# Own tile pools for meta tokens and rotary queries, the latents' ends behind the next projection's first products, the FFN norm's squares through PSUM

## The chip, the cores and the metric

The kernel runs on one core of one Trainium2 chip. The metric is the device time of the core in microseconds (us), from the program's first to its last instruction and what lies around it; the time before is the median of three runs.

## What is computed

One layer of an encoder with two token mixers. 1024 tokens and 16 learned meta tokens (1040 rows of width 1024, float32) pass a mixer and a gated feed-forward net (FFN):

```python
proj = u @ w_in
rq, rk, rv, rg, a_cq, a_ckv, a_kr, a_gret, a_gmla = jnp.split(proj, SPLIT_IDX, axis=-1)
y_ret = (silu(rg) * group_norm(bidir_retention(rope(rq), rope(rk), rv))) @ w_ret_out
c_q  = rmsnorm(a_cq, q_norm_w);   q = c_q @ w_uq            # 384-wide latent, 8 heads of 64 + 32 rotary
c_kv = rmsnorm(a_ckv, kv_norm_w); k_nope = c_kv @ w_uk; v = c_kv @ w_uv    # 256-wide latent
k_rope = rope(a_kr)                                          # one 32-wide key for all heads
y_mla = softmax_attention(q, [k_nope, k_rope], v) @ w_mla_out
merged = sigmoid(a_gret) * y_ret + sigmoid(a_gmla) * y_mla
h = h + merged @ w_o
h = h + (silu(u2 @ w_gate) * (u2 @ w_up)) @ w_down           # u2 = rmsnorm(h), d_ff = 2816
out = rmsnorm(h)[:, 16:]
```

## The kernel before

Everything lies with channels on the 128 partitions and tokens along the free axis. A float32 product is made of three matmuls on operands split into a high and a low part (hi·hi, hi·lo, lo·hi; lines L137 to L139, L217). The parts are made by ScalarE (the high copy, L209, L153, L275) and VectorE (the difference, L210, L154, L276).

**Units of seven products.** A product of 256 weight columns pairs with the two token halves goes by seven instead of eight block products (`seven`, `seven_out`; names 11, t2, t3, n1, 21, t4, 22). GpSimd makes the weights' sums (L191 to L193, L207), ScalarE and VectorE split them (L209, L210), TensorE runs 12 matmuls of 128x512 for each of the seven, and VectorE adds the PSUM banks up (L234 to L242). A unit has 84 matmuls. There are four banks (`pm`) for these products, so the next unit's t2 needs the bank of this unit's t2 read out.

**Stages the change touches**, in order of time: the units that make the values; those of the shared key and the third query latent (`project_key` on `win(22)`), of the key-value latent (`project_kv` on `win(20)`), and a gate unit of which one product was made at the start (`rest_gates`: it loads that from `e_d`, L813, and adds it at L302); then four units of the retention's output (`ret_out(0)` to `ret_out(3)`, on `Z`, whose blocks are loaded and split one by one at L839, L275, L276), which multiply by a gate that they load from `g_d` (`ret_post`, L856, L857) and store to `r_d` (L858). Around `ret_out(1)` and the third unit the rotary part of the queries is made: 36 matmuls from the normed query latents `cq` (loaded at L909), then the rotation on VectorE (L893 to L898). Within `ret_out(3)` the first pair of heads begins (`heads_k`, L973).

A latent's end is what follows its unit: the meta tokens' values, which gather in a PSUM tile of their own, are summed (`meta_sum`, L432), transposed on TensorE (L779 for the key-value latent, L802 for the shared key), split and stored (`latent_part`, L730, L732 to L734; `shared_key`, L755 to L763), and the sum of squares `lss` goes over the partitions by matmuls with ones (L160) into the norm's factor (`latent_norm`, L741 to L744).

Tiles of 128x512 come from a rotating pool `cr` of six slots: the units' sums, the meta tokens' small tiles (16 columns) and the rotary tiles alike.

**Output projection** (`w_o`): for each half c of the tokens and each of eight row blocks m, 24 matmuls (L137 to L139), the residual add from PSUM (L1216), and, for c = 1, the FFN's input blocks (L1229, L1234, L1236 on GpSimd, L1239, splits at L154). The square of the new residual is made by ScalarE (L1245) and added to `ssum` by GpSimd (L1246). `norm(c)` sums `ssum` over partitions by matmuls with ones (L1197). The FFN's first gate unit starts with nine matmuls of each of its first four products, which need row blocks 0 to 5 alone, and the last three of each follow.

Instructions keep their order on each engine; between engines they wait on semaphores. The order is made by the framework's scheduler from the order of the program and its priorities, and all DMAs of this kernel are issued from one queue, SP's, in order; an issue that waits holds the ones behind it.

## Time and profile before

| | us |
|---|---|
| median of three runs (1775.68 to 1776.03) | 1775.89 |
| the profiled execution, its own time | 1780.81 |
| its span, first to last instruction | 1779.0 |
| TensorE busy in it | 1714.6 (96%) |
| VectorE busy | 1339.0 (75%) |
| ScalarE busy | 861.1 (48%) |
| GpSimd busy | 790.1 (44%) |

The profile is of one execution. TensorE (PE) is busy for nearly all of it, so a shorter time comes from its idle stretches and from stretches in which its granted clock (PEclk, as a share of 2.4 GHz) was below 1. DVE is VectorE, ACT ScalarE, POOL GpSimd, SP the engine whose queue issues DMAs. A busy TensorE issues a 128x512 matmul every 0.22 to 0.23 us at full clock; the 0.39 us that a row shows is the time one spends in the pipeline.

### The profile page before, as it was taken

The page shows a single profiled execution, that of the slowest core. Times are in us where ns is not written, and L with a number is a line of the kernel's source. Part 1 is how long each engine was busy: PE and PEld are TensorE (multiplying, and loading weights), DVE is VectorE, ACT ScalarE, POOL GpSimd, SP SyncE. Part 2 cuts the span into 40 slices and gives each one's busy share as a digit, 9 for nine tenths or more (in the row PEclk, how much of TensorE's full clock was granted, in tenths as well). Part 3 has the DMA queues.
Part 4 walks back from the last instruction along what each step waited for, and adds up shares of the span by engine and source line. Part 5 has one row for each costly group of instructions (what it writes and reads, how often), then busy time and mean ns, then how long its engine had stood idle before and what let it go on. Part 6 is the DMA issues. An engine that isn't in the chain of part 4 may idle for free.

```text
span 1779.0 us, 26433 instructions
## 1 busy us (share of the span) xinstructions
PE 1714.6 (96%) x8804; PEld 1443.9 (81%) x8804; DVE 1339.0 (75%) x2448; ACT 861.1 (48%) x1614; POOL 790.1 (44%) x605
## 2 busy tenths in 40 slices
PE   8999999999999899999999999899999999999997
PEld 6788777788887677899998888788888888787787
DVE  7845778788888857888888758767666666987965
ACT  7425766344324523788787346433332232543434
POOL 1322257674554321234332524666676566533422
PEclk9999999999999899999999999999999999999999
DMA  7733823566546785111112754233323333854512
GB/s 255 240 101 119 295 85 117 180 201 213 189 158 230 213 301 179 28 34 40 30 59 69 231 187 162 66 101 119 101 95 101 107 105 101 286 176 123 154 57 95
DMA packets 145433, 253.59 MB, mean 143 GB/s; under 512 B 18889, under 2 KB 36738, under 8 KB 145298
## 3 DMA queue, kind: packets, MB, share of 16 engines
q1 hardware_dynamic: 145298, 251.92, 43.5%
q8 instruction: 69, 1.13, 0.3%
q14 instruction: 66, 0.54, 0.1%
HBM read 174.93 MB, written 76.85 MB: 142 GB/s over the span
## 4 chain that ended last, share of the span: by engine, by line
PE 49%; DVE 7%; DMA 3%; ACT 3%; issue 2%; SPq 0%; POOL 0%; DVEq 0%; ACTq 0%; POOLq 0%
PE mm L217 29%; PE o L1041 3%; PE mm L138 3%; PE mm L137 3%; PE mm L139 3%; PE t L1012 2%; DVE slot L154 2%; PE s L137 1%; PE s L138 1%; PE s L139 1%; DMA slot<-g_d 1%; DMA slot<-f_d 1%; DVE slot L210 1%; DVE ptl L1015 1%; PE o L137 1%
## 5 line engine op out<-in xcount | busy, mean ns | idle before, releaser
L217 PE MATMUL mm<-slot,slot 128*128 128x512 f32 x2604 | 598.3, 392 | 8.4 <-ACT slot L209 3.7
L217 PEld LDWEIGHTS mm<-slot,slot 128*128 128x128 f32 x2604 | 490.6, 189 | 115.0 <-DVE slot L210 5.5
L209 ACT CAST slot<-slot 128x512 fp32r<-128x512 f32 (+1 forms) x413 | 246.1, 598 | 465.9 <-PE mm L217 395.0
L210 DVE TENSOR_TENSOR slot<-slot,slot 128x512 fp32r<-128x512 f32 (+1 forms) x413 | 361.6, 877 | 71.5 <-ACT slot L209 70.4
L217 PE MATMUL mm<-ht,slot 128*128 128x512 f32 x648 | 219.6, 400 | 7.4 <-DVE slot L210 3.4
L217 PE MATMUL mm<-h,slot 128*128 128x512 f32 x536 | 184.4, 403 | 0.0
L191 POOL TENSOR_TENSOR slot<-slot,slot 128x512 f32<-128x512 f32 (+1 forms) x61 | 85.3, 1398 | 220.0 <-DMA slot<-in_w_u 50.7
L207 POOL TENSOR_TENSOR slot<-slot,slot 128x512 f32<-128x512 f32 (+1 forms) x61 | 84.7, 1390 | 185.1 <-DVE slot L210 173.1
L217 PEld LDWEIGHTS mm<-ht,slot 128*128 128x128 f32 x648 | 122.1, 190 | 35.1 <-DVE slot L210 5.6
L154 DVE TENSOR_TENSOR slot<-slot,slot 128x512 fp32r<-128x512 f32 x137 | 117.5, 872 | 20.6 <-ACT slot L153 20.0
L217 PE MATMUL mm<-lt,slot 128*128 128x512 f32 x324 | 128.7, 397 | 0.0
L153 ACT CAST slot<-slot 128x512 fp32r<-128x512 f32 x137 | 83.3, 619 | 76.9 <-DMA slot<-f_d 30.3
L192 POOL TENSOR_TENSOR slot<-slot,slot 128x512 f32<-128x512 f32 (+1 forms) x61 | 86.0, 1410 | 77.6 <-DVE slot L210 65.6
L217 PEld LDWEIGHTS mm<-h,slot 128*128 128x128 f32 x536 | 101.2, 190 | 21.6 <-DVE slot L210 0.6
L1002 DVE TENSOR_SCALAR_CACHE_REDUCE pr<-s,sq_c 128x384 f32<-128x384 f32 (+1 forms) x192 | 103.3, 573 | 7.9 <-PE t L1020 3.8
L217 PE MATMUL mm<-l,slot 128*128 128x512 f32 x268 | 106.6, 398 | 0.0
L139 PE MATMUL mm<-slot,slot 128*128 128x512 f32 (+1 forms) x288 | 105.3, 366 | 0.0
L138 PE MATMUL mm<-slot,slot 128*128 128x512 f32 (+1 forms) x288 | 105.3, 366 | 0.0
L137 PE MATMUL mm<-slot,slot 128*128 128x512 f32 (+1 forms) x288 | 105.1, 367 | 0.0
L1015 DVE TENSOR_TENSOR ptl<-t,pth 128x512 fp32r<-128x512 f32 x128 | 85.7, 685 | 18.2 <-ACT pth L1014 17.6
L1046 POOL TENSOR_TENSOR oa<-oa,ob 64x256 f32<-64x256 f32 x32 | 24.0, 751 | 154.5 <-ACT ob L1045 149.1
L193 POOL TENSOR_TENSOR slot<-slot,slot 128x512 f32<-128x512 f32 (+1 forms) x61 | 88.2, 1445 | 1.4
(365 smaller groups left out, 3506.0 us busy)
## 6 DMA issues: line engine op xcount, KB each, us to landing
slot<-in_w_in SPq DMA_DIRECT2D x106, 256.0 KB
f_d<-slot SPq DMA_DIRECT2D x71, 256.0 KB
slot<-f_d SPq DMA_DIRECT2D x71, 256.0 KB
slot<-in_xT SPq DMA_DIRECT2D x48, 256.0 KB
slot<-z_d SPq DMA_DIRECT2D x44, 256.0 KB
slot<-in_w_g SPq DMA_DIRECT2D x44, 256.0 KB
slot<-in_w_u SPq DMA_DIRECT2D x44, 256.0 KB
slot<-in_w_dq SPq DMA_DIRECT2D x48, 192.0 KB
```

What stands on the lines that cost most here:

```text
L137: pe.matmul(ps, sh, mh, start=start, stop=False)
L138: pe.matmul(ps, sh, ml, start=False, stop=False)
L139: pe.matmul(ps, sl, mh, start=False, stop=stop)
L154: dve.tensor_sub(lo, t, f(hi))
L191: pool.tensor_add(s1, a21, a22)
L192: pool.tensor_sub(s2, s1, a11)
L193: pool.tensor_sub(a21, a21, a11)
L209: act.copy(hi, side[b])
L210: dve.tensor_sub(low, side[b], f(hi))
L217: pe.matmul(ps, sw[:, ks], sx, start=begins and q == qs[0] and i == 0, stop=q == nq - 1 and i == 2, skip_group_check=True)
L1002: dve.tensor_scalar(pr[:, c], ps[:, :n], sq_c[:, qb : qb + 1], None, ALU.mult, ALU.max, accum_out=mx[:, j : j + 1])
L1015: dve.tensor_sub(pt[1][d], tp, f(pt[0])[d])
```

## The change

1. The meta tokens' tiles of up to 16 columns and their sums get pools of their own (`small`, 8 tiles; `sums`, 2 tiles); the rotary tiles get `rotary_r` (11 slots). `cr` keeps its six slots.
2. The end of the shared key's unit is written behind the products 11 and t2 of the key-value unit, that unit's end behind t2 and n1 of the gate unit.
3. The query latents' loads are tied to earlier stores; the key-value latents' tiles `ckv` and the factor row `skv_b` are opened and loaded after the third unit (in memory that the rotary pools leave), where they were loaded with the query latents before; a GpSimd memset goes.
4. For `w_o`, the squares go to a PSUM bank of the pool `pm` and are added by VectorE (14 adds move from GpSimd), the difference L1236 moves from GpSimd to VectorE (4), `norm(0)` is written after both halves, and `norm(1)` after the first 36 matmuls of the FFN's first unit.

```diff
@@ prod: products already written are not written again
-        banks, w, begun = {}, {}, []
+        banks, w, begun, done = {}, {}, [], set()
         def prod(b, qs=range(nq)):
             k = BANK[b]
+            qs = [q for q in qs if (b, q) not in done]
+            done.update((b, q) for q in qs)
@@ small tiles of the meta tokens
+        small, sums = sb(mid, "small", 8, side="right"), sb(mid, "sums", 2, side="right")
+        def work(n):
+            return slot(cr) if n > NM else mk(small, (P, NM), "small")
         def meta_sum(ps, lo, n):
-            t = slot(cr)[:NM, :n]
+            t = mk(sums, (P, 256), "sums")[:NM, :n]
...
         def latent_part(t, c, dst, col, first):
-            hi = slot(cr, F32R)[:, :n]
+            hi = work(n).bitcast(F32R)[:, :n]
...
@@ ends of the latents
         tail = slice(S, L)
+        pending = []
+        def after_pending(prod, names=("t2", "n1")):
+            if pending:
+                for b in names:
+                    prod(b)
+                pending.pop()()
+            return prod
         def project_kv():
...
-            seven_out(seven(w7, win(20), U, (ps, M1 | M2)), cr, post)
-            t = meta_sum(ps, 0, 256)
-            pt = mk(pc, (P, 512), "mm")
-            for k in range(2):
-                pe.transpose(pt[:, k * NM : k * NM + NM], t[:, k * P : k * P + P], ident[:NM, :NM])
-                latent_part(pt[:, k * NM : k * NM + NM], tail, ckv_d[k], column(C_KVN + k), k == 0)
-            latent_norm(skv_c, 2, 1.0, range(NB + 1))
+            seven_out(after_pending(seven(w7, win(20), U, (ps, M1 | M2)), ("11", "t2")), cr, post)
+            def rest():
+                t = meta_sum(ps, 0, 256)
...
+                latent_norm(skv_c, 2, 1.0, range(NB + 1))
+            pending.append(rest)
...
-            seven_out(seven(w7, win(22), U, (ps, M2)), cr, post)
-            t = meta_sum(ps, P, 48)
...
+            seven_out(after_pending(seven(w7, win(22), U, (ps, M2))), cr, post)
+            def rest():
+                t = meta_sum(ps, P, 48)
...
+                latent_norm(sq_c, 3, 96.0**-0.5, range(NB))
+            pending.append(rest)
...
         def rest_gates(i):
             e = slot(cr)
             load(e, e_d[i])
-            rest_out([(seven(w7, win(12 + i), U), e, gate_post(g_d, 2 * i))], cr)
+            rest_out([(after_pending(seven(w7, win(12 + i), U)), e, gate_post(g_d, 2 * i))], cr)
@@ rotary queries
-        ckv = [tuple(mk(ap, (P, 1152), f"ck{j}{k}", F32R)[:, :L] for j in "hl") for k in range(2)]
-        swp = sb(right, "skv", 1, side="right")
-        skv_b = mk(swp, (P, L), "skv_b")
-        fill(swp, 112)
...
+        rr_ = sb(rot, "rotary_r", 11, side="right")
...
-            ta, tb_ = slot(cr), slot(cr)
+            ta, tb_ = slot(rr_), slot(rr_)
...
-        for i, (dst, src) in enumerate([(t, cq_d[k][j]) for k in range(3) for j, t in enumerate(cq[k])] + [
-                (t, ckv_d[k][j]) for k in range(2) for j, t in enumerate(ckv[k])]):
-            with tc.issue_after(issued[1 + i * 3 // 5].ins):
+        for i, (dst, src) in enumerate([(t, cq_d[k][j]) for k in range(3) for j, t in enumerate(cq[k])]):
+            with tc.issue_after(issued[1 + i // 2].ins):
                 load(f(dst), src)
...
-        load(skv_b, n_d.rearrange("b i -> (b i)")[:L].unsqueeze(0).broadcast_to([P, L]))
...
         rot.close()
+        ap = sb(right, "latent_kv", 1, side="right")
+        ckv = [tuple(mk(ap, (P, 1152), f"ck{j}{k}", F32R)[:, :L] for j in "hl") for k in range(2)]
+        swp = sb(right, "skv", 1, side="right")
+        skv_b = mk(swp, (P, L), "skv_b")
+        load(skv_b, n_d.rearrange("b i -> (b i)")[:L].unsqueeze(0).broadcast_to([P, L]))
+        for k in range(2):
+            for j, t in enumerate(ckv[k]):
+                load(f(t), ckv_d[k][j])
         ret_out(3)
@@ output projection and the FFN's first unit
-                    pool.tensor_sub(g12, g12, g22)
+                    dve.tensor_sub(g12, g12, g22)
...
-                    t = slot(xr)
+                    t = mk(pm, (P, 512), "mm")
                     act.square(t, hm)
-                    pool.tensor_add(ssum[c], ssum[c], t)
-            norm(c, slice(0, 512))
+                    dve.tensor_add(ssum[c], t, ssum[c])
+        norm(0, slice(0, 512))
...
             if j == 0:
                 for b in NAMES[:4]:
                     prod(b, range(3))
-                    rest[b] = range(3, 4)
+                norm(1, slice(0, 512))
```

Three places in the order of the instructions. **TensorE between the gate unit and `ret_out(0)`**: `mm_1158` (`mm_1183` after) holds the key-value latent's transposed meta tokens, `mm_1164` (`mm_1189` after) the sums over `lss`, `mm_1191` is the gate unit's bank for t3, and `mm_1283` and `mm_1286` (`mm_1277` after) are banks of `ret_out(0)`. Before, behind `ret_out(0)`'s product 11:

```order
L217 MATMUL mm_1283_6157<-h11_1117_5602,slot_1285_6159 128x512
L779 MATMUL mm_1158_5813<-ident_2_63,slot_1157_5810 128x16
L160 MATMUL mm_1164_5832<-ones_3_68,lss_212_846 16x1
L217 MATMUL mm_1286_6175<-ht2_1166_5852,slot_1287_6176 128x512
L217 MATMUL mm_1286_6175<-lt2_1167_5853,slot_1287_6176 128x512
L217 MATMUL mm_1286_6175<-ht2_1166_5852,slot_1288_6177 128x512
```

After, the first transpose and half of the sums, at the start of the gate unit's t3:

```order
L219 MATMUL mm_1179_5872<-hn1_123_462,slot_1181_5874 128x512
L798 MATMUL mm_1183_5892<-ident_2_63,sums_1182_5889 128x16
L219 MATMUL mm_1191_5932<-ht3_145_570,slot_1192_5933 128x512
L219 MATMUL mm_1191_5932<-lt3_146_571,slot_1192_5933 128x512
L160 MATMUL mm_1189_5911<-ones_3_68,lss_212_852 128x1 x4
L219 MATMUL mm_1191_5932<-ht3_145_570,slot_1193_5934 128x512
```

and the other half at the end of that product:

```order
L219 MATMUL mm_1191_5932<-lt3_152_586,slot_1192_5933 128x512
L219 MATMUL mm_1191_5932<-ht3_151_585,slot_1193_5934 128x512
L160 MATMUL mm_1189_5911<-ones_3_68,lss_212_852 128x1 x4
L798 MATMUL mm_1183_5892<-ident_2_63,sums_1182_5889 128x16
L219 MATMUL mm_1277_6158<-h11_1100_5554,slot_1278_6159 128x512
```

The second transpose and the last sum stood between `ret_out(0)`'s products 11 and t2, where nothing else of TensorE's was between them; they stand apart now, with ten matmuls of t3 between the halves.

**VectorE at the start of `ret_out(1)`**, where `ret_out(0)`'s results (`slot_1299`, `slot_1281` before; `slot_1293`, `slot_1275` after) are multiplied by the gates (L857 before, L882 after) and `ret_out(1)`'s weights are split (L210 before, L212 after). Before:

```order
L240 TENSOR_TENSOR slot_1299_6253<-mm_1289_6193,slot_1281_6155 128x512
L210 TENSOR_TENSOR slot_1319_6332<-slot_1311_6306,slot_1318_6331 128x512
L242 TENSOR_TENSOR slot_1281_6155<-slot_1281_6155,mm_1292_6211 128x512
L210 TENSOR_TENSOR slot_1322_6350<-slot_1307_6298,slot_1321_6349 128x512
L857 TENSOR_TENSOR slot_1302_6271<-slot_1299_6253,slot_1302_6271 128x512
L857 TENSOR_TENSOR slot_1305_6293<-slot_1281_6155,slot_1305_6293 128x512
L210 TENSOR_TENSOR slot_1325_6368<-slot_1310_6305,slot_1324_6367 128x512
L234 TENSOR_TENSOR slot_1312_6310<-mm_1317_6330,slot_1312_6310 128x512
```

After:

```order
L212 TENSOR_TENSOR slot_1313_6333<-slot_1305_6307,slot_1312_6332 128x512
L882 TENSOR_TENSOR slot_1296_6272<-slot_1293_6254,slot_1296_6272 128x512
L212 TENSOR_TENSOR slot_1316_6351<-slot_1301_6299,slot_1315_6350 128x512
L244 TENSOR_TENSOR slot_1275_6156<-slot_1275_6156,mm_1286_6212 128x512
L905 TENSOR_TENSOR ql_1333_6456<-slot_1331_6453,qh_1332_6455 128x384
L882 TENSOR_TENSOR slot_1299_6294<-slot_1275_6156,slot_1299_6294 128x512
L212 TENSOR_TENSOR slot_1319_6369<-slot_1304_6306,slot_1318_6368 128x512
L905 TENSOR_TENSOR xl_1336_6462<-slot_1334_6459,qr_1335_6461 128x384
L236 TENSOR_TENSOR slot_1306_6311<-mm_1311_6331,slot_1306_6311 128x512
```

The multiplications by loaded gates now stand one by one between the splits of the weights, and the splits of the rotary weights (L905) among them. **SP's queue there.** Before:

```order
L915 DMA skv_b_1269_6129<-n_d_21_91 128x1040
L858 DMA r_d_12_82<-slot_1295_6229 128x512
L858 DMA r_d_12_82<-slot_1298_6249 128x512
L909 DMA cqh0_1259_6116<-cq_d_23_93 128x1024
L856 DMA slot_1302_6271<-g_d_14_84 128x512
L856 DMA slot_1305_6293<-g_d_14_84 128x512
L909 DMA cql0_1260_6117<-cq_d_23_93 128x1024
```

After:

```order
L883 DMA r_d_12_82<-slot_1289_6230 128x512
L883 DMA r_d_12_82<-slot_1292_6250 128x512
L881 DMA slot_1296_6272<-g_d_14_84 128x512
L881 DMA slot_1299_6294<-g_d_14_84 128x512
L930 DMA cqh0_1259_6124<-cq_d_23_93 128x1024
L901 DMA slot_1331_6453<-in_w_uq 128x384
L901 DMA slot_1334_6459<-in_w_uq 128x384
L930 DMA cql0_1260_6125<-cq_d_23_93 128x1024
```

The factor row `skv_b` is gone from here (it follows the third unit), and the gates stand ahead of the query latents.

**TensorE at the FFN's first unit** (`mm_2796` and on are its banks before, `mm_2793` and on after; `r3` is the norm's). Before:

```order
L217 MATMUL mm_2796_12461<-slot_2636_11888,slot_2797_12462 128x512
L217 MATMUL mm_2796_12461<-slot_2637_11889,slot_2797_12462 128x512
L217 MATMUL mm_2796_12461<-slot_2636_11888,slot_2798_12463 128x512
L217 MATMUL mm_2799_12475<-slot_2779_12414,slot_2800_12476 128x512
L217 MATMUL mm_2799_12475<-slot_2780_12415,slot_2800_12476 128x512
L217 MATMUL mm_2799_12475<-slot_2779_12414,slot_2801_12477 128x512
L1197 MATMUL r3_2788_12435<-ones_3_68,ssum1_2447_11114 128x1 x4
```

After:

```order
L219 MATMUL mm_2802_12504<-slot_2728_12242,slot_2803_12505 128x512
L219 MATMUL mm_2802_12504<-slot_2729_12243,slot_2803_12505 128x512
L219 MATMUL mm_2802_12504<-slot_2728_12242,slot_2804_12506 128x512
L1225 MATMUL r3_2805_12518<-ones_3_68,ssum1_2446_11128 128x1 x4
L219 MATMUL mm_2793_12462<-slot_2635_11902,slot_2794_12463 128x512
L219 MATMUL mm_2793_12462<-slot_2636_11903,slot_2794_12463 128x512
L219 MATMUL mm_2793_12462<-slot_2635_11902,slot_2795_12464 128x512
```

The sums over `ssum1` stood behind six of the twelve last matmuls of the first four products; they stand ahead of all twelve now. **VectorE there**, from the residual add of the last row block (L1216 before, L1244 after):

```order
L1216 TENSOR_TENSOR slot_2776_12407<-mm_2775_12382,slot_2774_12380 128x512
L210 TENSOR_TENSOR slot_2807_12505<-slot_2794_12456,slot_2806_12504 128x512
L1234 TENSOR_TENSOR slot_2778_12411<-slot_2777_12410,slot_2764_12358 128x512
L154 TENSOR_TENSOR slot_2780_12415<-slot_2778_12411,slot_2779_12414 128x512
L1239 SCALAR_TENSOR_TENSOR slot_2778_12411<-slot_2647_11934,cols_6_74,slot_2778_12411 128x512
L154 TENSOR_TENSOR slot_2782_12420<-slot_2763_12357,slot_2781_12419 128x512
```

After:

```order
L1244 TENSOR_TENSOR slot_2773_12408<-mm_2772_12383,slot_2771_12381 128x512
L212 TENSOR_TENSOR slot_2804_12506<-slot_2791_12457,slot_2803_12505 128x512
L1262 TENSOR_TENSOR slot_2775_12412<-slot_2774_12411,slot_2761_12359 128x512
L1264 TENSOR_TENSOR slot_2760_12358<-slot_2760_12358,slot_2774_12411 128x512
L1274 TENSOR_TENSOR ssum1_2446_11128<-mm_2784_12433,ssum1_2446_11128 128x512
L154 TENSOR_TENSOR slot_2777_12416<-slot_2775_12412,slot_2776_12415 128x512
```

The subtraction L1264 and the add L1274 out of PSUM have joined the row; of GpSimd's queue they are gone.

## Rows read from the trace of the kernel before

**Rows 1.** The page's busy times, shares of the span and instructions.
```profile
PE 1714.6 (96%) x8804; PEld 1443.9 (81%) x8804; DVE 1339.0 (75%) x2448; ACT 861.1 (48%) x1614; POOL 790.1 (44%) x605
```

**Rows 2.** Windows: length; busy PE, PEld, DVE, ACT, POOL; PEclk; DMA share; GB/s.
```profile
548.00:616.00 68.00, 56.59 (x257) 45.47 (x256) 56.85 (x91) 38.80 (x74) 25.37 (x18) 0.87 0.75 238
680.00:700.00 20.00, 16.00 (x65) 13.62 (x65) 14.84 (x24) 5.47 (x10) 4.60 (x6) 0.84 0.59 194
1120.00:1140.00 20.00, 17.20 (x71) 13.99 (x70) 14.81 (x18) 10.10 (x17) 13.34 (x10) 0.83 0.17 52
```

**Rows 3.** Waits of PE in 540 to 620: us in total, times, longest.
```profile
PE mm L217 <- DVE skv_c L744: 3.1, 1, 3.1
PE mm L160 <- DVE lss L730: 2.9, 1, 2.9
PE mm L779 <- DVE slot L432: 1.6, 1, 1.6
PE mm L217 <- DVE slot L210: 1.6, 2, 1.2
PE mm L802 <- DVE slot L432: 1.5, 1, 1.5
```

**Rows 4.** Waits of PE in 660 to 740.
```profile
PE t L137 <- DVE kf L973: 3.3, 1, 3.3
PE o L1041 <- ACT pth L1014: 1.9, 1, 1.9
```

**Rows 5.** Waits of PE in 1080 to 1140.
```profile
PE r L1197 <- POOL ssum L1246: 2.8, 1, 2.8
PE mm L217 <- DVE slot L210: 2.1, 1, 2.1
```

**Rows 6.** Waits of DVE in 548 to 616, the two longest.
```profile
DVE sq_c L741 <- PE mm L160: 2.2, 1, 2.2
DVE lt L276 <- ACT ht L275: 1.9, 1, 1.9
```

**Rows 7.** DVE's waits for gates in 600 to 720; timeline: start, us, what ran.
```profile
DVE slot L857 <- DMA slot<-g_d: 20.7, 7, 4.6
...
692.49 0.69 DVE L857 TENSOR_TENSOR slot<-slot,slot 128x512 f32<-128x512 f32 x1 [3.49 <-DMA slot<-g_d]
...
627.04 1.42 DVE L857 TENSOR_TENSOR slot<-slot,slot 128x512 f32<-128x512 f32 x2 [4.52 <-DMA slot<-g_d]
...
620.64 1.63 SPq L856 DMA_DIRECT2D slot<-g_d  x2
```

**Rows 8.** Windows: the values' units, and the first half of w_o.
```profile
145.00:219.00 74.00, 72.66 (x406) 57.50 (x406) 49.30 (x81) 49.37 (x99) 18.05 (x12) 1.00 0.69 225
1025.00:1060.00 35.00, 35.00 (x156) 29.01 (x155) 18.77 (x27) 16.70 (x27) 6.50 (x5) 1.00 0.54 188
```

**Rows 9.** Timeline of DVE and of SP's queue around the e_d load.
```profile
593.37 0.69 DVE L302 TENSOR_TENSOR slot<-mm,slot 128x512 f32<-128x512 f32 x1 [0.27 <-DMA slot<-e_d]
...
590.43 0.42 SPq L813 DMA_DIRECT2D slot<-e_d  x1
```

**Rows 10.** Timeline: DVE's residual adds of blocks 3 and 7; PE leaving block 7.
```profile
1088.01 0.69 DVE L1216 TENSOR_TENSOR slot<-mm,slot 128x512 f32<-128x512 f32 x1 [0.38 <-DMA slot<-in_xT]
...
1115.04 0.68 DVE L154 TENSOR_TENSOR slot<-slot,slot 128x512 fp32r<-128x512 f32 x1
1115.64 0.68 DVE L1216 TENSOR_TENSOR slot<-mm,slot 128x512 f32<-128x512 f32 x1
...
1108.39 4.70 PE L217 MATMUL mm<-slot,slot 128*128 128x512 f32 x20
```

**Rows 11.** Window from block 3's residual add to block 7's.
```profile
1088.00:1115.63 27.63, 25.55 (x113) 20.88 (x112) 25.96 (x28) 15.05 (x26) 16.90 (x10) 1.00 0.45 143
```

**Rows 12.** Groups of DVE in 1085 to 1120: count, busy, mean ns, idle before.
```profile
L154 DVE TENSOR_TENSOR slot<-slot,slot 128x512 fp32r<-128x512 f32 x12 | 10.8, 904 | 2.1 <-ACT slot L153 2.1
...
L1216 DVE TENSOR_TENSOR slot<-mm,slot 128x512 f32<-128x512 f32 x5 | 3.4, 684 | 0.4 <-DMA slot<-in_xT 0.4
```

More of the change, by code (lines that the diff above doesn't have):

```diff
@@ L570, in project_rope @@
                 x = meta_sum(ps, 0, 256).rearrange("t (h c) -> t h c", c=64)
-                y = slot(cr)[:NM, :256].rearrange("t (h c) -> t h c", c=64)
+                y = mk(sums, (P, 256), "sums")[:NM].rearrange("t (h c) -> t h c", c=64)
                 def table(i, lo, n):
@@ L727, in latent_part @@
             else:
-                q = slot(cr)[:, :n]
+                q = work(n)[:, :n]
                 act.square(q, t)
                 dve.tensor_add(lss[:, c], lss[:, c], q)
-            lo = slot(cr)[:, :n]
+            lo = work(n)[:, :n]
             dve.scalar_tensor_tensor(lo, t, col, f(hi), ALU.mult, ALU.subtract)
@@ L750, in shared_key @@
             n = c.stop - c.start
-            ca, sa = slot(cr)[:48, :n], slot(cr)[:48, :n]
+            ca, sa = work(n)[:48, :n], work(n)[:48, :n]
             load(ca, A["cM"][:48, c])
             load(sa, A["sM"][:48, c])
-            sb_, kh = slot(cr)[:48, :n], slot(cr, F32R)[:48, :n]
+            sb_, kh = work(n)[:48, :n], work(n).bitcast(F32R)[:48, :n]
             dve.tensor_mul(ks, ks, rstd_b[:48, c])
@@ L797, in post @@
                     shared_key(t[:48], half(name))
-            seven_out(seven(w7, win(22), U, (ps, M2)), cr, post)
-            t = meta_sum(ps, P, 48)
-            pt = mk(pc, (P, 512), "mm")
-            pe.transpose(pt[:48, :NM], t, ident[:NM, :NM])
-            ks = slot(cr)[:48, :NM]
-            act.copy(ks, pt[:48, :NM])
-            shared_key(ks, tail)
-            latent_norm(sq_c, 3, 96.0**-0.5, range(NB))
+            seven_out(after_pending(seven(w7, win(22), U, (ps, M2))), cr, post)
+            def rest():
+                t = meta_sum(ps, P, 48)
+                pt = mk(pc, (P, 512), "mm")
+                pe.transpose(pt[:48, :NM], t, ident[:NM, :NM])
+                ks = work(NM)[:48, :NM]
+                act.copy(ks, pt[:48, :NM])
+                shared_key(ks, tail)
+                latent_norm(sq_c, 3, 96.0**-0.5, range(NB))
+            pending.append(rest)
         def project_gates(i):
@@ L877, in wx_load @@
         def wx_load(i):
-            raw = slot(cr)[:, :384]
+            raw = slot(rr_)[:, :384]
             load(raw, A["w_uq"][4 + i])
@@ L888, in rotary @@
             if i == 0:
[L889 removed]
+                tables[:] = slot(rr_), slot(rr_)
                 load(tables[0], A["cM"][:, c])
                 load(tables[1], A["sM"][:, c])
[L892 removed]
+            ta, tb_ = slot(rr_), slot(rr_)
             dve.tensor_mul(ta, xx[lo, i], tables[0])
@@ L929, in build @@
         rot.close()
+        ap = sb(right, "latent_kv", 1, side="right")
[3 more added lines that the diff above has]
+        load(skv_b, n_d.rearrange("b i -> (b i)")[:L].unsqueeze(0).broadcast_to([P, L]))
+        for k in range(2):
+            for j, t in enumerate(ckv[k]):
+                load(f(t), ckv_d[k][j])
         ret_out(3)
```

4 lines of the change are left out of this document (3 added, 1 removed).

## The prediction

> **What bounds the kernel now.** The busy times come first [rows 1]: TensorE is busy for 1714.6 us of the 1779.0 of the span. All other engines have room on the average, VectorE with 1339.0 the least. What a change of order can win is therefore TensorE's 64.4 us of idle time and the time lost to a lower clock; the matmuls stay the same ones.
>
> Then the windows [rows 2]. They show where these losses lie that the change can reach: 548 to 616 (TensorE busy for 56.59 of 68.00 us, at a mean granted clock of 0.87), 680 to 700 (16.00 of 20.00, clock 0.84) and 1120 to 1140 (17.20 of 20.00, clock 0.83). I call these places A (ends of the latents), B (rotary queries and first heads) and C (output projection into the FFN). The row of A tells something that the share of the whole span hides: VectorE is busy there for 56.85 of the 68.00 us, as much as TensorE. Last, the waits: who ends TensorE's idle time in A [rows 3], in B [rows 4] and in C [rows 5], and what VectorE itself waits for in A [rows 6] and near B [rows 7].
>
> The sum is made against the profiled execution, whose own time is 1780.81; the median of the runs is 1775.89, that is 4.9 lower, and I take the same microseconds off the median.
>
> **Part 1, pools for the small tiles.** Meta tokens' tiles of 16 columns held slots of 128x512 in a pool of six. At the place where the values are made this reorders some work, yet there TensorE is busy for 72.66 of 74.00 us [rows 8]: at most 1.3 to win. I take 0, from -1 to +1. Its real use is with part 2.
>
> **Part 2, place A.** Before, the ends stood on TensorE between units: a transpose that waits for the meta tokens' sum (1.5 for the shared key, 1.6 for the key-value latent), the sums over lss (2.9), and then the next product t2 of ret_out(0) (3.1). The rows put this last one on skv_c [rows 3], but skv_c's row was only the last that the profile matched: t2 needs the bank that VectorE's L302 reads at 593.37, and L302 waited for the load from e_d, issued at 590.43 [rows 9], behind the stores of the latent's end in SP's queue. The change moves the ends behind products that are ready, and in the new order the e_d load precedes those stores, so both causes go. With the two waits for L210 (1.6) the listed waits are 10.7. The clock cost comes on top: (1 - 0.87) of 68.00 us is 8.8 [rows 2], less 1.5, half of the 3.1 that TensorE idled at the lower clock, so 7.3. At most 18.0.
>
> But VectorE's work does not shrink: the 56.85 us [rows 2] have to be done in A in any order, so the 68 us can shrink by at most 11.15. How much of that idle time goes? VectorE waited 2.2 for TensorE's sums (L741), which the change hides behind matmuls, and the waits behind ScalarE's copies of ret_out(0)'s blocks (1.9 the longest [rows 6]) hang on loads and copies that stay. So 2.2 should go for sure, and of the other 8.95 I take two fifths, 3.6, nearer to the kept end because those copies are most of it. **A: 5.8, bounds 2 and 11.**
>
> **Part 3, place B.** The wait of 3.3 [rows 4] was for kf (L973), the first head's keys, which stood in VectorE's queue behind L857, and that waited 3.49 for a gate from g_d [rows 7]. The heads' first products now stand behind ret_out(3)'s last, so 3.3 goes, and the clock's (1 - 0.84) of 20, 3.2 [rows 2], less 0.4 for idle time in it: 6.1. The wait of 1.9 for ScalarE's pth [rows 4] may stay; it and the clock's rest make the upper bound. What is late next? The rotary products now start inside ret_out(1), after its 11, t2 and t3 (36 matmuls of 0.227 each, 8.2 us: the 20 of one row last 4.70, of which the last one alone is 0.39 [rows 10]). They need the first query latent loads. Nearest row: the gate load of the same place, issued in a burst at 620.64, ended VectorE's wait at 627.04 [rows 7], 6.4 us later. A second latent load issued 2 us into the unit lands so at 8.4: a wait between 0 and some 2, and I charge 2, the upper end, because two more weight loads stand in the same stretch of SP's queue. On the other side the gates stand ahead of the latents there now, and skv_b (520 KB) is gone from ahead of them, so VectorE's waits of 4.6 get shorter. The later loads of ckv are free: their tiles are ready once the last rotation is stored, and some fifty matmuls of the third unit and 72 of ret_out(3) (over 25 us) lie between. **B: 4.1, bounds -1 and 9.**
>
> **Part 4, place C.** The two waits, 2.1 for a split and 2.8 for GpSimd's last add to ssum [rows 5], and the clock's (1 - 0.83) of 20, 3.4 [rows 2]: at most 8.3. What stands behind them is VectorE's lag. Block 3's residual add starts at 1088.01, block 7's at 1115.64; TensorE goes from block 7 to the FFN at 1108.39 [rows 10], so VectorE is 7.2 behind TensorE there. Its 28 instructions in between took 27.63 us [rows 11], but two undisturbed neighbours start 0.60 apart [rows 10]: they would take 16.8. I put the other 10.8 down to GpSimd's ten instructions there (16.90 busy), 1.08 each. In the changed order six more VectorE instructions (34, 20.4 us) and only four of GpSimd's (4.3 us) stand between: 24.7 against 21.8 of matmuls (4 blocks of 24 at 0.227). Block 3's residual add came 1.4 after its products (1088.01 against 1108.39 - 21.8 = 1086.6), so block 7's lag is 1.4 + 2.9 = 4.3 instead of 7.2. ssum's last add is the fourth instruction behind the residual add: it ends 4.3 + 4 of 0.60 + 0.7 = 7.4 after the block's products, and the norm's sums stand 36 matmuls, 8.2 us, behind them. So no wait, with a margin of 0.8; I leave 2.8 for ScalarE's part of the chain and a remnant of the clock. In the other half VectorE has room for the new adds (18.77 busy of 35.00 [rows 8]). **C: 5.5, bounds 2.3 and 8.3.**
>
> The row on which this rests: in the same stretch the residual add, with one input in PSUM, took 684 ns, and L154, with both in SBUF, 904 [rows 12], and a GpSimd instruction 16.90 / 10 = 1.69 us [rows 11]. The Trainium skill, page "SBUF — State Buffer", section "Who interferes with whom", says that a VectorE instruction with two SBUF inputs and a GpSimd instruction that reads SBUF block each other for the whole instruction, while one with at most one SBUF input is free of it. By that rule the ssum adds from PSUM stay short, as the row has it; but the four GpSimd instructions left would hold VectorE for their full 1.69 us, 2.4 more than I count, the norm would wait 1.6, and C would give some 3 instead of 5.5 if the clock fell as well. The 1.08 from the rows decides.
>
> **The rivals.** (a) VectorE and ScalarE as the next bound: in A only the small ends go (2 to 3), C's remnant is large (2.5), B gives 3: 8, so 1768. For it: VectorE is busy for 84% of A [rows 2]. Against: its own waits there were in part for TensorE. (b) All of it: A 11, B 9, C 8.3, 28 us: 1748. (c) The change moves waits without removing them, since each end has a VectorE chain that someone waits for: 1776. (d) Slower, by one mechanism: in ret_out(1) the gate multiplications stand ahead of the weight splits on VectorE, each waiting for a load. Before, seven such waits took 20.7 us [rows 7], and all but 3.5 of this cost TensorE nothing. If the rest now held the splits, 17.2 us would go to TensorE, and 1775.9 - 11.3 (A and C) + 17.2 gives 1781.8. It decides when a wait exceeds the lead of a split, some two products or 5.4 us; the longest was 4.6, and the gates are loaded earlier now.
>
> **How the numbers follow.** 5.8 + 4.1 + 5.5 = 15.4; 1775.9 - 15.4 = **1760.5** (for the profiled execution 1765.4). Chances: the forecast (1756 to 1766) 0.53, (a) to 1772.3 0.19, (b) 0.10, (c) 0.08, (d) 0.10. A measurement of this kernel tells some 0.2% (3.6 us) from no change: faster 0.82, same 0.08, slower 0.10. The range leaves out (d) and most of (c): 1748 to 1773.
>
> **What would show it.** Right: clock 1.00 and TensorE busy for over 97% of the stretch of A, C's norm sums without a wait for ssum, no wait for kf at B. Wrong: VectorE near 90% in A with TensorE still waiting for its splits (a); new waits of TensorE for a split behind L882, or for the query latents (d); half-clock stretches at the same three places although the waits have shrunk.

## The result

The changed kernel takes 1762.17 us, the median of six runs (1759.23 to 1766.91), the kernel before 1776.4 in the runs beside it: a ratio of 0.9917, 95% interval 0.9901 to 0.9933. That is 14.2 us less by the medians, where 15.4 were forecast. The profiled execution took 1763.15. It is 17.7 us under that of before, more than the medians: 3.7 us of this lie ahead of the three places (its 2521st matmul starts at 502.67, against 506.32 before). Most of that is not the change's: 2.8 us stand at the 181st matmul already, and in all runs below, with or without each part, the 2521st starts between 501.4 and 504.6. So the two profiles are compared by stretches and not by spans.

The first fence is the changed kernel's busy line and three windows (length; busy PE, PEld, DVE, ACT, POOL; PEclk; DMA share; GB/s): place A from the 2521st to the 3001st matmul, place B from there to the 3601st, place C from the 5301st to the 6001st. The second holds the same three stretches of the kernel before.

```profile
PE 1706.9 (97%) x8804; PEld 1437.4 (82%) x8804; DVE 1346.9 (76%) x2466; ACT 860.4 (49%) x1615; POOL 762.4 (43%) x586
...
502.67:607.12 104.45, 96.84 (x482) 76.70 (x481) 92.57 (x176) 50.92 (x94) 42.45 (x27) 0.95 0.62 202
607.12:731.01 123.89, 119.17 (x601) 100.33 (x600) 90.61 (x182) 53.59 (x101) 25.55 (x24) 0.99 0.58 195
972.66:1130.22 157.56, 155.82 (x701) 128.75 (x700) 119.97 (x166) 76.99 (x130) 47.64 (x33) 1.00 0.51 168
```

```profile
506.32:615.91 109.59, 97.82 (x482) 79.00 (x481) 93.72 (x179) 51.17 (x95) 43.73 (x28) 0.92 0.62 199
615.91:742.73 126.82, 119.63 (x601) 101.78 (x600) 88.93 (x177) 52.05 (x98) 24.91 (x24) 0.97 0.55 184
983.21:1147.02 163.81, 158.92 (x701) 131.30 (x700) 119.22 (x148) 77.69 (x130) 75.57 (x51) 0.98 0.49 162
```

A is 5.1 us shorter, B 2.9 and C 6.3. In C TensorE is idle for 1.74 us in all and the clock is 1.00 throughout; in A 7.6 us of idle time are left. Where it waits now, by the waits of the changed kernel in 535 to 620, 620 to 740 and 1060 to 1140 (us, times, longest), which answer to [rows 3], [rows 4] and [rows 5]:

```profile
PE mm L160 <- DVE lss L738: 4.2, 2, 2.6
PE mm L219 <- DVE slot L212: 2.1, 3, 1.0
PE mm L219 <- ACT slot L211: 1.2, 2, 0.8
PE mm L798 <- DVE small L740: 0.6, 1, 0.6
...
PE o L137 <- DVE slot L244: 2.1, 1, 2.1
PE mm L219 <- ACT slot L211: 0.9, 1, 0.9
...
PE r L174 <- DVE r2c L1230: 1.7, 1, 1.7
```

The waits for skv_c (3.1), for kf and for ssum are gone, and of those of the transposes (L779 and L802 before, 3.1 together) 0.6 is left. The sums over lss wait longer than before, 4.2 us in two places against 2.9, and in B and C a new wait of some 2 us each stands where a longer one stood. The granted clock stood at 0.50 in A from 557.0 to 560.4 and from 580.8 to 587.7, 10 us in all, where it had been 17 us before (557.0 to 563.8, 584.3 to 587.7, 591.1 to 598.0); in B it stood there for 3.4 us instead of 6.8, in C for none instead of 6.8.

C can be read in two timelines, VectorE's and TensorE's (start, us, what ran):

```profile
1102.36 0.68 DVE L1244 TENSOR_TENSOR slot<-mm,slot 128x512 f32<-128x512 f32 x1
1102.96 0.68 DVE L212 TENSOR_TENSOR slot<-slot,slot 128x512 fp32r<-128x512 f32 x1
1103.83 0.69 DVE L1262 TENSOR_TENSOR slot<-slot,slot 128x512 f32<-128x512 f32 x1 [0.19 <-ACT slot L1261]
1104.44 0.69 DVE L1264 TENSOR_TENSOR slot<-slot,slot 128x512 f32<-128x512 f32 x1
1105.04 0.68 DVE L1274 TENSOR_TENSOR ssum<-mm,ssum 128x512 f32<-128x512 f32 x1
1105.64 3.12 DVE L154 TENSOR_TENSOR slot<-slot,slot 128x512 fp32r<-128x512 f32 x2
1108.68 1.77 DVE L1267 SCALAR_TENSOR_TENSOR slot<-slot,cols,slot 128x512 f32<-128x512 f32 x1
1110.38 1.45 DVE L154 TENSOR_TENSOR slot<-slot,slot 128x512 fp32r<-128x512 f32 x2
1111.75 0.17 DVE L1230 RECIPROCAL r2c<-r2c 128x4 f32<-128x4 f32 x1
```

```profile
1097.85 8.58 PE L219 MATMUL mm<-slot,slot 128*128 128x512 f32 x36
1106.27 0.95 PE L1225 MATMUL r<-ones,ssum 128*128 128x1 f32 x8
1107.07 3.16 PE L219 MATMUL mm<-slot,slot 128*128 128x512 f32 x12
1111.97 0.71 PE L174 MATMUL r<-ident,r2c 128*128 128x128 f32 x4 [1.74 <-DVE r2c L1230]
```

TensorE leaves row block 7 at 1097.85 and VectorE begins its residual add at 1102.36, 4.5 us behind, where it was 7.2 [rows 10] and 4.3 were forecast. The last add to ssum ends at 1105.72, and the norm's sums start at 1106.27 with no wait. What is late next is the norm's reciprocal, which stands in VectorE's queue behind five instructions, of which the first three (3.12 for two of L154, 1.77 for L1267) ran beside three of GpSimd's (1105.22 to 1109.91): that is the wait of 1.74.

### The profile page after: what moved, and what is told of

Same layout as the page of the kernel before. It is cut to its first block, busy times and chain, and to the rows that moved or that the text cites. A ratio compares the mean times of both kernels' runs of the same rounds, so it can differ in the third digit from the quotient of the medians.

```text
span 1761.1 us, 26377 instructions
## 1 busy us (share of the span) xinstructions
PE 1706.9 (97%) x8804; PEld 1437.4 (82%) x8804; DVE 1346.9 (76%) x2466; ACT 860.4 (49%) x1615; POOL 762.4 (43%) x586
## 4 chain that ended last, share of the span: by engine, by line
PE 51%; DVE 5%; ACT 2%; issue 1%; DMA 1%; DVEq 0%; SPq 0%; ACTq 0%
PE mm L219 31%; PE o L1069 3%; PE mm L138 3%; PE mm L137 3%; PE mm L139 3%; PE t L1040 2%; DVE slot L154 1%; PE s L137 1%; PE s L138 1%; PE s L139 1%; DVE ptl L1043 1%; DMA slot<-f_d 1%; PE o L137 1%; PE o L139 1%; PE o L138 1%
## 5 line engine op out<-in xcount | busy, mean ns | idle before, releaser
L211 ACT CAST slot<-slot 128x512 fp32r<-128x512 f32 (+1 forms) x413 | 245.9, 598 | 470.1 <-PE mm L219 379.3
L212 DVE TENSOR_TENSOR slot<-slot,slot 128x512 fp32r<-128x512 f32 (+1 forms) x413 | 365.7, 887 | 71.7 <-ACT slot L211 71.2
L191 POOL TENSOR_TENSOR slot<-slot,slot 128x512 f32<-128x512 f32 (+1 forms) x61 | 83.7, 1372 | 301.2 <-DMA slot<-in_w_g 80.8
L154 DVE TENSOR_TENSOR slot<-slot,slot 128x512 fp32r<-128x512 f32 x137 | 113.0, 841 | 12.3 <-ACT slot L153 11.5
L192 POOL TENSOR_TENSOR slot<-slot,slot 128x512 f32<-128x512 f32 (+1 forms) x61 | 86.4, 1416 | 82.5 <-DVE slot L212 66.0
L193 POOL TENSOR_TENSOR slot<-slot,slot 128x512 f32<-128x512 f32 (+1 forms) x61 | 89.2, 1463 | 1.4
```

The costliest lines, as they stand in the source:

```text
L154: dve.tensor_sub(lo, t, f(hi))
L192: pool.tensor_sub(s2, s1, a11)
L193: pool.tensor_sub(a21, a21, a11)
L211: act.copy(hi, side[b])
L212: dve.tensor_sub(low, side[b], f(hi))
```

## The experiments

All ratios are to the kernel before in the runs of the same chip. The stretches A, B and C of each profiled execution, cut at the same matmuls, stand in one table:

| kernel | median us | ratio, 95% interval | A | B | C |
|---|---|---|---|---|---|
| before | 1776.4 | | 109.6 | 126.8 | 163.8 |
| changed | 1762.2 | 0.9917 (0.9901 to 0.9933) | 104.5 | 123.9 | 157.6 |
| pools_alone (part 1) | 1776.6 | 0.9996 (0.9984 to 1.0007) | 104.5 | 130.6 | 162.4 |
| ends_alone (parts 1, 2) | 1775.8 | 0.9992 (0.9983 to 1.0001) | 104.9 | 128.0 | 163.5 |
| rotary_alone (part 3) | 1776.9 | 1.0003 (0.9989 to 1.0017) | 112.1 | 123.0 | 161.7 |
| ffn_alone (part 4) | 1770.8 | 0.9963 (0.9950 to 0.9975) | 109.2 | 127.3 | 158.0 |
| no_ends (1, 3, 4) | 1762.2 | 0.9916 (0.9902 to 0.9930) | 104.4 | 121.2 | 157.7 |
| no_pools (2, 3, 4) | 1771.3 | 0.9973 (0.9961 to 0.9985) | 109.3 | 124.7 | 158.3 |
| rotary_in_six | 1772.9 | 0.9981 (0.9970 to 0.9991) | 104.4 | 132.5 | 159.4 |
| own_slot_before | 1773.5 | 0.9987 (0.9976 to 0.9998) | 109.0 | 124.5 | 162.9 |
| squares_in_sbuf | 1764.1 | 0.9924 (0.9912 to 0.9937) | 105.5 | 121.6 | 159.8 |
| three_more | 1764.7 | 0.9924 (0.9912 to 0.9936) | 104.6 | 120.7 | 158.3 |
| two_waits_less | 1763.6 | 0.9925 (0.9913 to 0.9938) | 104.3 | 123.2 | 159.7 |
| less_vector (one run) | 1771.1 | | 103.2 | 129.2 | 159.4 |

The columns A, B and C are of one execution each. Stretches that an edit leaves alone differ by 0.4 us in A and B between before and ffn_alone, but by 1.0 in A and 2.3 in B between the changed kernel and squares_in_sbuf; C lies between 161.7 and 163.8 in all kernels without part 4. So differences of 2 us and more are read in A, and of 3 and more in B and C.

**Each part by itself.** The first four apply the diff's parts one by one to the kernel before; pools_alone is the pools `small` and `sums` only, ends_alone adds the code that puts the ends behind products.

> The kernel before with parts 1 and 2 alone (small pools, the latents' ends behind the next unit's products); rotary queries and w_o as before. Theory, that the three places gain apart from each other: TensorE's place A (the stretch from the end of the value and core units to ret_out(1)) is 5.1 us shorter between the two profiled executions, so about 5 us under the kernel before, 1771, with the waits of 3.3 (kf) and 2.8 (ssum) still there. Rival, that place A gains only because the query latents' loads and the factor row leave SP's queue there (part 3): 0 to 2 us under before.

> The kernel before with part 3 alone (own pool for rotary tiles, key-value latents and factor row loaded after the third unit). Theory: place B is 1.6 us shorter between the two profiled executions, since the new wait of 2.1 for the value products and a clock stretch of 3.4 came in place of 3.3 and 6.8; so 1 to 2 us under before. Rival, that the sums are hidden by the noise of the two executions and the removed waits (3.3 + 0.7 + 0.7 and 3 us of clock) count in full: 5 us and more under before.

> The kernel before with part 4 alone (squares through PSUM and added by VectorE, one difference moved to VectorE, norm sums ahead of the last products). Theory: place C is 6.3 us shorter between the profiled executions and hangs on nothing else: 6 us under before, 1770. Rival, that C's waits were set by VectorE's lag that began earlier: under 3 us.

> The kernel before with part 1 alone: small tiles of the meta tokens in pools of their own, nothing moved by hand. Theory: 0 us, within 1.5 us of before, as place A waits for the ends' chains and not for slots. Rival, that the slots of the pool of six were what held the ends: 2 us and more under before, and then part 2 is not what wins.

The one line of each that matters most, in the order above (ends, rotary, FFN, pools):

```diff
+            seven_out(after_pending(seven(w7, win(22), U, (ps, M2))), cr, post)
...
+        rr_ = sb(rot, "rotary_r", 11, side="right")
...
+                    dve.tensor_add(ssum[c], t, ssum[c])
...
+            return slot(cr) if n > NM else mk(small, (P, NM), "small")
```

Part 4 behaves as forecast: 6.6 us by its ratio, all of it in C. The others do not add up: pools_alone 0.7, ends_alone, which has the pools in it, 1.4, and rotary_alone -0.5 us by their ratios; parts 1 to 3 so come to 1 of the 8 us that are left for them. The stretches tell why. pools_alone shortens A by the full 5.1 us and gives 3.7 of it back in B; ends_alone is no better in A. The waits of pools_alone in 612 to 740:

```profile
PE t L137 <- DVE kf L979: 3.2, 1, 3.2
PE mm L217 <- ACT h L275: 2.1, 1, 2.1
PE o L1047 <- ACT pth L1020: 1.9, 1, 1.9
```

kf and pth wait as before. rotary_alone wins 3.9 in B, and its A is 2.5 longer. With pools alone the scheduler, too, splits the sums over lss in halves between matmuls of the gate unit and issues the e_d load ahead of the latent's last stores: what part 2 writes by hand happened without it.

Where a slot was missing before, ScalarE's rows show. The copy that begins the end of the shared key's unit (L431 before, L439 after) takes a tile for the meta tokens' sum. Before it ran 47.5 us into A, after a wait for VectorE's L732. What it reads comes from TensorE, so what it waited for on VectorE was a slot to write to. In the changed kernel it ran 36.4 us into A. The three rows are of before, of the changed kernel and of no_pools (below), where the copy of the key-value latent waited 2.85 us:

```profile
553.84 0.19 ACT L431 COPY slot<-mm 16x48 f32<-16x48 f32 x1 [0.88 <-DVE slot L732]
...
539.05 0.19 ACT L439 COPY sums<-mm 16x48 f32<-16x48 f32 x1
...
579.06 0.36 ACT L438 COPY slot<-mm 16x256 f32<-16x256 f32 x1 [2.85 <-DVE slot L739]
```

In all nine kernels with part 1 this copy of the shared key's sum runs 36.4 us into A, and A is 103.2 to 105.5 long; in the five without it runs 46.5 to 48.1 us into A, and A is 109.0 to 112.1. No run moves the copy and nothing else.

**One part taken out of the changed kernel.** So the next two undo one part each.

```diff
-            seven_out(after_pending(seven(w7, win(20), U, (ps, M1 | M2)), ("11", "t2")), cr, post)
-            def rest():
...
+            seven_out(seven(w7, win(20), U, (ps, M1 | M2)), cr, post)
+            t = meta_sum(ps, 0, 256)
```

> The changed kernel without part 2: the latents' ends are written directly behind their units again, the pools of their own, the rotary part and w_o stay as changed. Theory, formed after pools_alone shortened place A by 5 us and lost it again in place B: the pools carry the gain of A (they let the scheduler place the ends and the e_d load earlier), and part 3 keeps it; so no loss, 1762 within 2 us. Rival, the prediction's: part 2 hides the ends; without it TensorE waits for the sums over lss and for skv_c again, 5 us more, 1767.

```diff
-            return slot(cr) if n > NM else mk(small, (P, NM), "small")
+            return slot(cr)
...
-            t = mk(sums, (P, 256), "sums")[:NM, :n]
+            t = slot(cr)[:NM, :n]
```

> The changed kernel without part 1: the meta tokens' small tiles and sums come from the pool of six slots again; ends behind products, rotary part and w_o as changed. Theory that the pools carry A's gain: 5 us more than the changed kernel, 1767, and the e_d load late in SP's queue. Rival, that writing the ends behind products suffices: 1762 within 2 us.

Without part 2 nothing is lost (0.9916 against 0.9917). Without part 1 the kernel takes 1771.3, 9 us more, and A is 109.3 long as before. The profiled execution of no_pools was its fastest (1767.5), so the stretches show A's 4.9 of these 9 us and not where the rest goes. The pools carry A; writing the ends behind products without them wins nothing there. One part of what was expected failed: the e_d load was not late in no_pools (575.86, against 575.47 in the changed kernel and 590.43 before), and A was long all the same.

**What part 3 needs.** In no_ends, the rotary tiles go back to the pool of six, and the late loads of the key-value latents stay:

```diff
-            ta, tb_ = slot(rr_), slot(rr_)
+            ta, tb_ = slot(cr), slot(cr)
```

> no_ends with the rotary tiles in the pool of six slots again; the key-value latents and the factor row stay loaded after the third unit. Theory, that part 3 keeps place A's gain by loading less before the third unit: 1762 within 2 us. Rival, that it keeps it by leaving the six slots to the units' sums and gates: 4 us more and over, 1766.

It takes 1772.9, some 11 us more than no_ends, and B is 11.3 longer. Its longest wait there, VectorE's timeline, the issue that it waited for, and what that issue waited for:

```profile
PE t L137 <- DVE slot L898: 7.3, 1, 7.3
...
671.09 0.69 DVE L897 TENSOR_TENSOR slot<-mm,slot 128x512 f32<-128x512 f32 x1 [3.50 <-DMA slot<-in_cM]
...
668.16 0.33 SPq L894 DMA_DIRECT2D slot<-in_cM  x1
...
SPq L894 <- DMA r_d<-slot: 2.6, 1, 2.6
```

The rotation's tables found a slot only at 668.16, when the store of a result to r_d had left it; the rotation reads the rotary products from PSUM, so the banks came free late, and the first heads' keys waited 7.3 us for one. The rival was right: part 3 keeps A's gain by its slots, not by loading less.

**Is the e_d load A's cause?** The kernel before, with a tile of its own for the gate unit's stored product:

```diff
+        eo = sb(mid, "eo", 1, side="right")
...
-            e = slot(cr)
+            e = mk(eo, (P, 512), "eo")
```

> The kernel before with one edit: the gate units' stored product (loaded from e_d) gets a tile of its own and not a slot of the pool of six. Theory, that the pools won place A by letting this load go early: place A (from the core units' end to ret_out(1)) 3 to 5 us shorter between the profiled executions, of which place B gives most back, so 1774 to 1777. Rival, that the small tiles' slots as such held the ends: place A within 1 us of the kernel before.

No: the load now goes at 516.63, and A is 109.0, so the rival was right. The wait of 3.1 for the bank is gone, and one of 3.5 for L311, the next reading of a bank, stands 10 us further on; L311 stood in VectorE's queue behind the latent's factor (L744), which waited 2.55 us for ScalarE. By its ratio the kernel is 0.13% under before, just clear of its interval.

**Where the square lies.**

```diff
-                    t = mk(pm, (P, 512), "mm")
+                    t = slot(xr)
```

> The changed kernel with the squares of the output projection's results in an SBUF slot as before; VectorE still adds them, now with both inputs in SBUF. Theory, that C's gain is the work taken off GpSimd: within 1.5 us of the changed kernel, 1762 to 1764. Rival, by the rule on the shared port: the adds stretch beside GpSimd's four instructions, VectorE's lag at the last row block grows by 3 us, and the norm's sums wait: 1765.

The median is 1.9 us over the changed kernel's, 1.2 by the ratios, and the intervals overlap: between the theory's 1.5 and the rival's 3 the time does not decide. C is 2.2 longer, with 1.8 us of short waits. The adds themselves, in 1066 to 1112, of the changed kernel and of this one (busy, mean ns):

```profile
L1274 DVE TENSOR_TENSOR ssum<-mm,ssum 128x512 f32<-128x512 f32 x7 | 4.8, 681 | 0.0
```

```profile
L1274 DVE TENSOR_TENSOR ssum<-ssum,slot 128x512 f32<-128x512 f32 x7 | 5.9, 840 | 0.0
```

With both inputs in SBUF the seven are 1.1 us longer in sum, and one of them makes it: the last, which began beside a GpSimd instruction that ran from 1103.38 to 1105.02. Out of PSUM none is longer, but that is hardly a test: of those seven only the last overlapped GpSimd (from 1105.22), and it had begun before. The rival could not show either, since the scheduler put the norm's sums behind more products here (1110.81, where they stood at 1106.27):

```profile
1103.78 1.78 DVE L1274 TENSOR_TENSOR ssum<-ssum,slot 128x512 f32<-128x512 f32 x1
...
1110.81 1.15 PE L1225 MATMUL r<-ones,ssum 128*128 128x1 f32 x8 [0.38 <-ACT rs_b L177]
```

That C's gain is the work taken off GpSimd fits this run, with 4.0 us of the gain left, but no run parts it from the new places of the two norms. The new place of norm(1)'s sums alone cannot be it: they stand six matmuls nearer to the last row block than before.

**At the waits that are left.** three_more puts the ends one product further behind (names ("11", "t2", "t3") and ("t2", "n1", "t3")), has ret_out(3) written so that it reads its last bank before the third result is multiplied by its gate, and writes norm(1)'s spread later; two_waits_less, on no_ends, has the second of these and ties the spread behind the FFN's fifth product.

```diff
-            seven_out(after_pending(seven(w7, win(20), U, (ps, M1 | M2)), ("11", "t2")), cr, post)
+            seven_out(after_pending(seven(w7, win(20), U, (ps, M1 | M2)), ("11", "t2", "t3")), cr, post)
...
-            seven_out(seven(w7, A["w_ro"][j], Z), cr, ret_post(j))
+            seven_out(seven(w7, A["w_ro"][j], Z), cr, ret_post(j), late=j == 3)
...
-                norm(1, slice(0, 512))
+                tail = norm(1, slice(0, 512), later=True)
```

> The changed kernel and three edits at waits that its profile shows: ret_out(3) reads its last bank before it multiplies its third result by a gate (the value products waited 2.1 for that, with 3.4 us at half clock behind it); the latents' ends stand one product further behind (the sums over lss waited 2.6 and 1.6); norm(1)'s spread stands behind one product more (waited 1.7). Theory, that these waits are TensorE's alone: 2.1 + 1.7 + 4 + 1.7 of them, less what the next wait takes, 6 to 8 us under the changed kernel, 1755. Rival, that VectorE bounds place A (90% busy): only 3 to 4 us, 1758.

```diff
                     if name == "11":
-                        tail()
+                        with tc.issue_after(lastmm[0].ins):
+                            tail()
                         gate_post("22", first[0])
```

> no_ends with two edits at waits: ret_out(3) reads its last bank before it multiplies its third result by a gate (2.1 and a half-clock stretch of 3.4 us, 1.7 of it lost), and norm(1)'s spread is tied behind the FFN's fifth product (1.7). Theory, that both waits are TensorE's alone: 4 to 5 us under no_ends, 1757.5. Rival, that VectorE's queue is late by as much at the next product: within 1.5 us of no_ends.

Neither is faster than the changed kernel. In three_more A's waits for lss fall from 4.2 to 0.5, and TensorE waits 4.3 for a copy of weights (L211) instead; A keeps its length. The wait in C stays, as the scheduler left the spread where it was. In two_waits_less the spread did move, and TensorE waited 2.1 us for the reading of a bank (ScalarE's L237) one product ahead of it.

The edit to ret_out(3) is in neither order: in both kernels VectorE still multiplies by the gate before it reads the last bank, in two_waits_less at L870 before L247:

```profile
682.53 0.69 DVE L870 TENSOR_TENSOR slot<-slot,slot 128x512 f32<-128x512 f32 x1 [3.97 <-issue]
683.14 0.68 DVE L247 TENSOR_TENSOR slot<-slot,mm 128x512 f32<-128x512 f32 x1
```

So the value products still waited 1.8 there. In three_more they do not wait, with the same order: the gate's load was issued at 675.87, where it is 679.55 in the changed kernel, and the multiplication began 4.4 us sooner. Whether the other order would win anything is untested.

**Is VectorE A's bound?**

```diff
+                if nm in NAMES[4:]:
+                    Z[q][nm] = hi, hi
```

> The changed kernel with the low parts of 16 of the 28 blocks of Z left out (their high parts are used twice, so the retention's output is less exact): 16 VectorE subtractions, about 10 us of work, fewer in and behind place A, TensorE's matmuls the same. If VectorE bounds A: TensorE's waits from the gate unit on (some 5 us and a clock stretch) go, 4 us and more less between the key's unit and ret_out(1). Rival, that ScalarE's copies and the loads of Z bound it: under 1.5 us.

With the high part used twice, these products hold weight high times block high two times, so the output is far off the layer's and not only less exact; the matmuls are the same in number and shape. The edit took out 12 subtractions (three of the seven names by four blocks), not 16. VectorE is busy for 88.08 us in A instead of 92.57, and A is 1.3 us shorter, little more than what A differs by anyway. By what was expected that speaks for the copies and loads. But only some seven of the subtractions lie in A, at its end, and the kernel's order changed behind it (B is 5 us longer), so it doesn't settle the question.

## Why the prediction was right, and where not

- **The sum.** 15.4 were forecast, 14.2 measured, by places 5.8, 4.1 and 5.5 against 5.1, 2.9 and 6.3. Every place lies within its bounds. That the sum came so near is in part luck: A's gain comes from another part than the one it was credited to, B's from a charge that fell elsewhere, and C's lag from errors that offset each other, as told below.
- **The signs.** Of the signs of being right, no wait for ssum and none for kf came true. That of A did not: TensorE is busy for 93% of the stretch and not 97, at a clock of 0.95. The sign of rival (a) showed instead: VectorE is busy for 89% of A (92.57 of 104.45), and TensorE waits for its splits three times (L212, 2.1 us). A's gain lies above the 2 to 3 us of (a) all the same.
- **Part 1 was the step that failed.** It was costed at 0 ("-1 to +1") from the stretch where the values are made, and its real use was put with part 2. Alone it is worth 0.04%, so that number holds; but taken out of the changed kernel it costs 9 us. A's 5.1 us come from it, with or without part 2, and B's part 3 is of the same kind: slots of the pool of six. The prediction saw the small tiles sit in full slots and didn't ask who waited for a slot. The rows that it read, TensorE's waits, name none; a missing slot shows where the slot is to be filled, at ScalarE's copy (0.88 and 2.85 above) or as a load that is issued late (in_cM at 668.16). The e_d load, which the prediction held to be one cause of A, was late (590.43 [rows 9]), but A is as long where it goes early (no_pools, own_slot_before).
- **Part 2 was credited with A and does nothing.** The prediction read the new order, where the ends stand apart between matmuls, as the work of the code that writes them there. no_ends shows the halves of the key-value latent's sums in the same order from the scheduler alone, and in no_pools, which has that code, the sixteen stand in a row again. Nor did the wait for lss go, as the sum had it: it grew from 2.9 to 4.2.
- **A's bound.** Of the 11 us that VectorE's work leaves in [rows 2], half was taken. With own pools A is 104.3 to 105.5 us in all kernels but less_vector, wherever the ends stand, with different waits each time. That fits the prediction's view, and rival (a)'s, that the next engines are close behind; which of VectorE, ScalarE's copies and the loads holds it is open.
- **B.** kf's wait went as said. The charge of 2 for the first rotary products was wrong: no wait for the query latents shows; it fell instead on the value products, 2.1, for a bank whose reading (L244) stands in VectorE's queue behind a multiplication by a gate:

```profile
684.00 0.69 DVE L882 TENSOR_TENSOR slot<-slot,slot 128x512 f32<-128x512 f32 x1 [4.30 <-issue]
684.61 0.68 DVE L244 TENSOR_TENSOR slot<-slot,mm 128x512 f32<-128x512 f32 x1
```

  The profile names no releaser for these 4.30 us; that it is the gate's load is read from its issue at 679.55, and from three_more, where the wait of the same instruction is put down to g_d. That is the mechanism of rival (d), at another place and for 2 us, not 17.
- **C.** The lag of 4.5 against 4.3, the last add's end 7.9 us behind the block's products against 7.4, no wait for ssum: these steps hold. What the lag is made of was off both ways. Block 3's residual add began 0.75 us behind its products (1097.85 - 21.8 = 1076.05) and not 1.4, the 34 instructions from there took 25.6 us and not 24.7, GpSimd lengthened them by 2.9 and not 4.3, and VectorE stood idle for 1.45, which the sum had left out:

```profile
1076.80 0.69 DVE L1244 TENSOR_TENSOR slot<-mm,slot 128x512 f32<-128x512 f32 x1 [0.92 <-DMA slot<-in_xT]
```

  The remnant of 2.8 was 1.7, a wait for the reciprocal, and the clock came back in full.
- **The rule on the shared port.** By it C was to give 3. It gave 6.3. The four GpSimd instructions between the residual adds of block 3 (1076.80) and block 7 (1102.36) ran for 6.1 us and lengthened VectorE's by 2.9: L1262, L1264 and L1257 took 1.51, 1.78 and 1.73 us, where they take 0.69, 0.68 and 0.75 elsewhere in the stretch, and the first of the four cost nothing, as VectorE waited for a load or read PSUM for most of it:

```profile
1087.81 1.31 POOL L191 TENSOR_TENSOR slot<-slot,slot 128x512 f32<-128x512 f32 x1 [76.57 <-DMA slot<-in_w_g]
1089.20 1.79 POOL L192 TENSOR_TENSOR slot<-slot,slot 128x512 f32<-128x512 f32 x1
1090.96 1.73 POOL L193 TENSOR_TENSOR slot<-slot,slot 128x512 f32<-128x512 f32 x1
1097.59 1.30 POOL L209 TENSOR_TENSOR slot<-slot,slot 128x512 f32<-128x512 f32 x1 [4.90 <-DVE slot L212]
```

```profile
1088.55 0.69 DVE L1244 TENSOR_TENSOR slot<-mm,slot 128x512 f32<-128x512 f32 x1 [0.58 <-DMA slot<-in_xT]
...
1090.03 1.51 DVE L1262 TENSOR_TENSOR slot<-slot,slot 128x512 f32<-128x512 f32 x1 [0.19 <-ACT slot L1261]
1091.46 1.78 DVE L1264 TENSOR_TENSOR slot<-slot,slot 128x512 f32<-128x512 f32 x1
...
1097.70 1.73 DVE L1257 SCALAR_TENSOR_TENSOR slot<-slot,cols,slot 128x512 f32<-128x512 f32 x1 [0.20 <-ACT slot L1256]
```

  The Trainium skill, page "SBUF — State Buffer", section "Who interferes with whom", calls the ports that VectorE and GpSimd share an exclusive lock, from which a VectorE instruction with at most one SBUF input is free. The trace agrees: L1244 reads PSUM, began at 1088.55 in the midst of GpSimd's L191 and took 0.69; and each of the three long ones ends 0.54 to 0.55 us behind the GpSimd instruction beside it, as if held to that one's end. What failed is the price that the prediction drew from it, the whole 1.69 us of each GpSimd instruction. VectorE came to its instructions partway, GpSimd was itself drawn out (L192 and L193, 1.79 and 1.73, where L191 took 1.31), and the first met no instruction to hold: 0.7 us each, against 1.08 from [rows 11] and [rows 12].

## What to carry to other kernels

Count who holds slots of a shared rotating pool before moving code by hand: a tile that finds no slot delays the copy or the load that is to fill it, the profile shows that there and not at TensorE, and a pool of its own can be worth more than a new order. Take each part out of the changed kernel, not only into the old one: here parts 1 and 3 were worth nothing alone and 8 us together (no_ends against ffn_alone, by their ratios). When a queue is late by a few us at one wait, look at the next one before pricing its removal: of the edits at remaining waits two took effect, the ends one product further behind and the spread behind the fifth product, and each moved the wait and won nothing. And read the order of a run before its time: the other edits at these waits left the order as it was.

## What was unexpected of the hardware

Tiny VectorE instructions stretch beside GpSimd as much as large ones: in the changed kernel a 16x16 multiplication took 1.15 us and the next 1.20, where the same two took 0.16 and 0.17 before, in idle time of GpSimd. Each ends 0.02 to 0.03 us behind the GpSimd instruction beside it, the rows of which stand below. An instruction on 16x16 numbers can so hold up the queue for as long as two of 128x512:

```profile
551.16 1.15 DVE L765 TENSOR_TENSOR small<-small,small 16x16 f32<-16x16 f32 x1
552.35 1.20 DVE L766 TENSOR_TENSOR small<-small,small 16x16 f32<-16x16 f32 x1
...
551.01 1.28 POOL L712 TENSOR_TENSOR slot<-slot,slot 128x512 f32<-128x512 f32 x1
552.25 1.27 POOL L191 TENSOR_TENSOR slot<-slot,slot 128x512 f32<-128x512 f32 x1
...
559.79 0.16 DVE L757 TENSOR_TENSOR slot<-slot,slot 16x16 f32<-16x16 f32 x1
559.98 0.17 DVE L758 TENSOR_TENSOR slot<-slot,slot 16x16 f32<-16x16 f32 x1
```
